# A macaron encoder block: another scheduling clock at a hand-over, five late tiles instead of four, the last norm's weights through another queue, and an uncut last piece

## The chip, the cores and the metric

The kernel runs on one core of a Trainium2 chip. The metric is the device time of one execution in microseconds (us), lower is better. The engines are TensorE (PE, matmuls; PEld is its weight load), VectorE (DVE), ScalarE (ACT), GpSimd (POOL) and SyncE (SP, which here only issues DMAs). Each runs its instructions in the order of its queue and waits there by semaphores.

## The reference

One layer on 1024 tokens of width 1024, in float32: a gated feed-forward half step, a mixer of three branches (sparse attention, a state-space layer, attention into a memory) that are gated, summed and projected, a second gated half step, and a last norm.

```python
x = x + 0.5 * swiglu_ffn(rms_norm(x, ffn1_norm[l]), ffn1_w_in[l], ffn1_w_out[l])
h = rms_norm(x, mix_norm[l])
...
x = x + merged @ w_out[l]
x = x + 0.5 * swiglu_ffn(rms_norm(x, ffn2_norm[l]), ffn2_w_in[l], ffn2_w_out[l])
x = rms_norm(x, final_norm[l])
```

`swiglu_ffn` is `(silu(h @ gate) * (h @ up)) @ w_out`, with 2816 hidden channels.

## The kernel before

**Matmuls.** The activations lie with channels on partitions; `xa` holds x, 8 tiles of 128 channels by 1024 tokens, in two halves of 512 tokens. Each matmul operand is a float16 number and a float16 remainder, and a product is three matmuls (`matmul3`, line 930).

**Weights.** A weight block is loaded into one of two float32 buffers (`wf`) by SP's queue. ACT squares it (`junk`, whose row sums are `wss`), PE adds these across partitions (`ms<-wss,ones_b`), DVE makes a scale of it (`wsc`), ACT writes the scaled float16 copy and DVE the remainder (both `wh`). Only then is `wf` free for the next load but one. `WBlock.steps` (line 235) is this list; `Stream.prep` puts the steps between the matmuls, each where an order's clock says that its engine has time.

**The order's clock.** `Model` (line 70) adds up a cost for every instruction as it is written, by engine and size (`cost`, line 102), and keeps from it a time per engine and per piece of memory. `Sched` and `Stream.prep` decide by these times what is written next, so costs and due times here move instructions in each engine's order, while the chip then runs the order as it stands. `WBlock.LATE` is how many us after its squares a block's sum over partitions may come. Tiles named in `nc.free` are left out of the clock; `xa` is among them during the mixer.

**The hand-over.** The mixer's output stage (`out_stage`, line 1165, called at line 2368) has 16 units of 24 matmuls, one per tile d of 128 channels and half of the tokens; DVE adds x to each (`xa<-mm`), ACT squares it (`sq`). `tail_order(8, 4)` takes both halves of tiles 0 to 3, then half 0 of tiles 4 to 7, then their half 1, so that half 0 is complete four units before the end. The generator `norm_forms` (line 865) then makes that half's norm, in four pairs of `xa<-xa,gs,ao` on DVE, and the float16 forms `F` and `FB` on ACT, DVE and POOL. The second FFN's `ffn_strassen` (line 1012) begins with six heads, three blocks of weights by two halves, of 96 matmuls of 256 columns each. Beside the heads, norm_forms makes sums of quarters of x (`xa<-xa`) and their forms. After them, 19 blocks go through a Strassen product; the sums of their weights (`wsum`) are POOL's. `ffn_strassen` sets the clock for this body behind the head loop:

```python
rows.apart, self.stream.BACKLOG = True, 2.0
nc.ACC, WBlock.LATE = {"scalar": 0.25, "vector": 0.08}, 1.0
```

**The end.** The last output stage (`out_stage` at line 2538) multiplies the FFN's hidden tiles (`H`, and the last ones in `xa`) with `w_out`. `final` (line 2372) turns each result back to tokens by rows (transposes into `lg`), multiplies it with the norm's weights (`F<-lg,xa`; the weights lie in a piece of `xa`, loaded by ACT's queue at line 2535), and after the last tile makes the root and scales the rows, which SP's queue stores 128 at a time. The last unit is cut in two pieces of 256 tokens (`cut=(0, HT // 2, HT)`); its 33 products are made twice with 256 columns, and root, scaling and stores follow each piece for two groups of 128 rows.

Of the kernel before, what the change touches and what calls it, by code (L numbers as in the profile page):

```python
# [17 lines left out]
P = 128  # L18
S = 1024
D = 1024  # L20
ND = D // P
HT = 512
# [29 lines left out]
class Engine:  # L52


    def __init__(self, model, name, engine):
        self.model, self.name, self.engine = model, name, engine
# [13 lines left out]
class Model:  # L70
# [6 lines left out]
    def __init__(self, nc):  # L77
        self.nc = nc
        self.t = {n: 0.0 for n in self.ENGINES}
        self.dma, self.end = 0.0, 0.0  # L80
        self.wrote, self.used, self.last, self.slots, self.ring, self.free = {}, {}, {}, {}, {}, set()
        for n in self.ENGINES:
            setattr(self, n, Engine(self, n, getattr(nc, n)))
# [18 lines left out]
    def cost(self, e, op, out, ins, acc):  # L102
        size = lambda a: a.free_size()
        n = max([size(out)] + [size(a) for a in ins]) if e != "tensor" else size(out)
        ptrs = sum(1 for a in ins[1:] if size(a) == 1 and n > 1)
        if e == "tensor":
            c = (n / 2400 + 0.0025) * (1 if ins[0].dtype != F32 else 4)
            return max(0.026, c * (0.6 if out.shape[0] <= 64 else 1.0))
        if e == "scalar":
            return 0.07 + n * 0.833e-3 + 0.093 * ptrs  # L110
        if op == "reciprocal":
            return 0.07 + 6.3e-3 * n
        sbuf = all(a.space == bass.MemoryType.SB for a in [out] + ins)
        fast = 0.52e-3 if op in ("tensor_scalar", "tensor_copy", "memset") and sbuf and not acc else 1.042e-3
        if e == "gpsimd":
            return 0.13 + n * (3.64e-3 if op == "tensor_scalar" else 2.0e-3)
        return 0.065 + n * fast + 0.061 * ptrs
# [269 lines left out]
class SBlock(WBlock):  # L387
# [40 lines left out]
    def sum(self):  # L428
        kb, nc, i = self.kb, self.kb.nc, self.summed
        H = self.HALF  # L430
        end, nc.end = nc.end, 0.0
        self.s[i] = kb.sums.tile([P, 2 * H], F32, name="wsum", tag=f"wsum{i}")
        x, y = self.s[i][:, 0:H], self.s[i][:, H:2 * H]
        sub = lambda o, a, b: nc.gpsimd.tensor_tensor(o, a, b, op=OP.subtract)
        if i == 0:
            nc.gpsimd.tensor_tensor(x, self.a(2), self.a(3), op=OP.add)
            sub(y, x, self.a(0))
        else:
            sub(x, self.a(0), self.a(2))
            sub(y, self.a(1), self.s[0][:, H:2 * H])  # L440
        self.summed += 1
        self.sums_at[i], nc.end = nc.end, end
# [162 lines left out]
class Builder:  # L605
# [406 lines left out]
    def ffn_strassen(self, name, rows, a, b, F, ring, early, chunks, xd):  # L1012
# [4 lines left out]
        nc = self.nc  # L1017
# [10 lines left out]
        def begin(f, c, tiles, gt):  # L1028
            w = a[f]
            yield from self.stream.begin(w, "head")  # L1030
            v = lambda g, j: g.rearrange("p (h a t) -> p a h t", h=2, a=2)[:, j, c.start // C:c.stop // C]
            return dict(w=w, c=c, gt=[v(gt, j) for j in range(2)], **dict(zip(("a", "u2", "u3", "si"), tiles)))
# [8 lines left out]
        def m1(s):  # L1041
            s["b1"] = self.mm()
            product(s, "b1", "A11", "B11", False)
            nc.scalar.activation(s["a"], s["b1"][:, s["c"]], AF.Copy)
# [69 lines left out]
        for i, (f, half) in enumerate(self.head_order(PLAIN)):  # L1114
            if i in (0, 2):
                yield f"h{name}.{half}"
            w = a[f]
# [16 lines left out]
                rows.put(f, gts[f])  # L1134
                rows.flush()
        rows.apart, self.stream.BACKLOG = True, 2.0
        nc.ACC, WBlock.LATE = {"scalar": 0.25, "vector": 0.08}, 1.0
        ends = [r1 for _, r1 in chunks[:-1]]

        def first(f):  # L1140
            if f == PLAIN:
                for half in range(2):
                    yield f"f{name}.{half}"
            gt = ring("gt")
            s = yield from begin(f, whole, [ring("post") for _ in range(4)], gt)
            m1(s)
            s["row"] = f, gt
            yield None
            return s
# [1061 lines left out]
    def mixer(self, w, xa, ss, xd_in, xd_out, after):  # L2211


        nc, tc, sched = self.nc, self.tc, self.sched
# [97 lines left out]
        for n in range(2 * ND):  # L2312
# [5 lines left out]
            gb, ga = self.bank("lg"), self.mm()  # L2318
# [43 lines left out]
        xo, F = after()  # L2362
        pool = m3.enter_context(tc.tile_pool(name="xo4", bufs=1, side="right"))
        xo = xo + [pool.tile([P, HT], F32, name="xo4", tag=f"xo4{i}") for i in range(3)]
        xo = iter([xo[i % len(xo)] for i in range(2 * ND)])
        for h in range(2):
            sched.add(self.norm_forms(xa, h, lambda h=h: self.row_sums(ss[h]), 2, "3", F), 0)
        yield from self.out_stage(w["out"], w["m"], lambda: next(xo), xd_in, 2, 4, self.keep_x("3", xa, ss, xd_out), 4)
        m3.close()

    def final(self, xt, ss, gb, out):
# [48 lines left out]
def tile_hybrid_block(ctx, tc, x, mem, ffn1_norm, ffn1_w_in, ffn1_w_out, mix_norm, w_in, a_q_gain, a_k_gain, rel_bias,  # L2420
# [4 lines left out]
    kb = Builder(ctx, tc)  # L2425
    nc, const, sched, stream = kb.nc, kb.const, kb.sched, kb.stream
    ctx.enter_context(kb.psum("ps", 2, 3, 2, 1))
    xa = const.tile([P, ND, 2, 2, HT // 2], F32, name="xa")
    nc.free.add(xa.tensor.name)
    ss = [const.tile([P, HT], F32, name=f"ss{h}") for h in range(2)]  # L2430
    xd = [kb.dram.tile([ND, 2, P, HT], F32, name=f"xd{i}") for i in range(3)]
# [7 lines left out]
    g1, g2 = Rows(kb, NF, "G"), Rows(kb, NF, "H")  # L2439
    a1, b1 = kb.ffn_blocks(ffn1_w_in[0], ffn1_w_out[0], 0, g1)  # L2440
    a2, b2, order2 = kb.sblocks(ffn2_w_in[0], ffn2_w_out[0], 2, g2, chunks)
# [45 lines left out]
    def main():  # L2487
        yield from kb.ffn_in("1", pa, a1, g1, xa, before)
        for h in range(2):
            sched.add(kb.norm_split(xa, h, lambda h=h: kb.row_sums(ss[h]), 1, "2"), 0)  # L2490
        xo = lambda: pa.tile([P, 2, HT], F32, name="xo", tag="gt", bufs=2)[:, 0]
        yield from kb.out_stage(b1, g1, xo, xd[0], 1, 2, kb.keep_x("2", xa, ss, xd[1]))
        st.close()
        with ExitStack() as en:
            F = {}

            def after():
                pool = en.enter_context(tc.tile_pool(name="g3", bufs=1, reuse_waits="tile"))
                F["pool"], F["B12", 0] = pool, pool.tile([P, ND // 2, 2, HT // 2], F16, name="FB12", tag="wsum1")
                names = ("B11", "B21", "B22", "T1", "T2", "T3", "T4")  # L2500
                F["all"] = pool.tile([P, len(names), ND // 2, 2, HT], F16, name="F")
                for i, n in enumerate(names):
                    F[n] = F["all"][:, i]
                F["xo"] = [pool.tile([P, HT], F32, name="xo3", tag=f"xo3{i}") for i in range(4)]
                return F["xo"], F

            yield from kb.mixer(mw, xa, ss, xd[1], xd[2], after)
            nc.free.discard(xa.tensor.name)
            pool = en.enter_context(tc.tile_pool(name="g4", bufs=1, reuse_waits="tile"))
            F["B12", 1] = pool.tile([P, ND // 2, 2, HT // 2], F16, name="FB12", tag="H7")  # L2510
            tiles = xa.rearrange("p k a h t -> p (k a h t)").rearrange("p (i t) -> p i t", t=HT)
            n = {"post": 0, "gt": 0, "xo": 0}

            def ring(kind):
                n[kind] += 1
                i = n[kind] - 1
                if kind == "xo":
                    return F["xo"][i % 4]
                if kind == "gt":
                    i = 8 + 2 * (i % 2)  # L2520
                    return tiles[:, i:i + 2].rearrange("p i t -> p (i t)")
                return tiles[:, i % 8]

            def room(k):
                k %= chunks[0][1]
                if k > 8:
                    i = 12 + 2 * (k - 9)
                    return tiles[:, i:i + 2].rearrange("p i t -> p (i t)").bitcast(F16).rearrange("p (j t) -> p j t", j=2)
                return pool.tile([P, 2, S], F16, name="H", tag=f"H{k}")

            g2.room = room
            early = lambda f: pool.tile([P, 2 * HT], F32, name="early", tag=f"H{4 + f}")
            yield from kb.ffn_strassen("3", g2, a2, b2, F, ring, early, chunks, xd[2])
            gb = tiles[:, 8:10].rearrange("p i t -> p (i t)")
            nc.scalar.dma_start(gb, final_norm.to_broadcast([P, D]))
            xt = F["all"].rearrange("p n k j t -> p (n k j t)").bitcast(F32)[:, 0:S * D // P].rearrange("p (i n) -> p i n", n=D)
            done, between = kb.final(xt, ss, gb, out[0])
            yield from kb.out_stage(b2[-1], g2, lambda: ring("xo"), xd[2], 2, 2, done, 3, cut=(0, HT // 2, HT), between=between)
            between()

    sched.add(setup(), 1)
    sched.add(main(), 3)
    sched.run()

# [29 lines left out]
```

## Time and profile before

| | |
|---|---|
| median of 3 runs | 2273.84 us (2272.67 to 2274.34) |
| the profiled execution | 2275.79 us, of which its span is 2273.9 |
| mean granted clock of PE | 0.980 |
| busy share of the span | PE 95%, DVE 60%, ACT 52%, POOL 18% |
| second output stage of the mixer and heads | about 1480 to 1659 us |
| Strassen body | 1659 to 1820 and 1937 to 2123 us, between them the first half of the second output product |
| last output stage and norm | 2123 to 2273.9 us |

Times in the rows are us from the start of the span. A row of a timeline has start, duration, engine, the line that emitted it (all go through a helper at line 62), operation, output tile<-inputs and shapes; in brackets the engine's idle time before it and what ended that. Buffer numbers are left out of names there. A row "x12" groups 12 like instructions, its duration is from the first's start to the last's end.

### The profile page before, as it was taken

The page shows a single profiled execution, that of the slowest core. Times are in us where ns is not written, and L with a number is a line of the kernel's source. Part 1 is how long each engine was busy: PE and PEld are TensorE (multiplying, and loading weights), DVE is VectorE, ACT ScalarE, POOL GpSimd, SP SyncE. Part 2 cuts the span into 40 slices and gives each one's busy share as a digit, 9 for nine tenths or more (in the row PEclk, how much of TensorE's full clock was granted, in tenths as well). Part 3 has the DMA queues.
Part 4 walks back from the last instruction along what each step waited for, and adds up shares of the span by engine and source line. Part 5 has one row for each costly group of instructions (what it writes and reads, how often), then busy time and mean ns, then how long its engine had stood idle before and what let it go on. Part 6 is the DMA issues. An engine that isn't in the chain of part 4 may idle for free. (4 is left out here: it accounts for less than half of the span.)

```text
span 2273.9 us, 33537 instructions
## 1 busy us (share of the span) xinstructions
PE 2155.2 (95%) x12618; PEld 1154.3 (51%) x12622; DVE 1353.6 (60%) x3682; ACT 1187.5 (52%) x2368; POOL 399.1 (18%) x581
## 2 busy tenths in 40 slices
PE   7999999999999889979999999898999999999897
PEld 4555444444444556666566674344844444444344
DVE  6446853345555476768669876775746643566553
ACT  6543433344444488778877675544445432455421
POOL 1200130000000014302200005400434301344000
PEclk9999999999999999989999999998999999999998
DMA  6422231202222112123322123244011233112212
GB/s 222 121 86 79 58 102 56 63 26 84 88 88 84 47 32 68 45 64 121 124 68 76 48 69 129 101 146 133 2 55 56 70 125 121 47 56 63 88 54 93
DMA packets 204067, 185.20 MB, mean 81 GB/s; under 512 B 7376, under 2 KB 176528, under 8 KB 203264
## 3 DMA queue, kind: packets, MB, share of 16 engines
q1 hardware_dynamic: 185904, 135.84, 18.9%
q0 software_dynamic: 8272, 28.84, 3.9%
q10 hardware_dynamic: 9728, 18.38, 2.6%
q8 instruction: 99, 1.62, 0.3%
q14 instruction: 64, 0.52, 0.1%
HBM read 143.57 MB, written 40.50 MB: 81 GB/s over the span
## 5 line engine op out<-in xcount | busy, mean ns | idle before, releaser
L62 PEld LDWEIGHTS <-wh 128*128 128x128 f16 x8445 | 824.8, 99 | 954.9 <-issue 41.1
L62 PE MATMUL mm<-xa,wh 128*128 128x512 f16 x2382 | 541.1, 380 | 6.5 <-ACT xa L62 4.9
L62 PE MATMUL lg<-xa,wh 128*128 128x512 f16 x1080 | 244.2, 381 | 0.4 <-DVE xn L62 0.4
L62 ACT ACTIVATE junk<-wf 128x1024 f16<-128x1024 f32 (+3 forms) x292 | 193.9, 664 | 39.3 <-DMA wf<-in_ffn_w_in_dram 22.3
L62 PE MATMUL mm<-G,wh 128*128 128x512 f16 x960 | 210.5, 379 | 0.0
L62 DVE SCALAR_TENSOR_TENSOR wh<-wf,wsc,wh 128x1024 f16<-128x1024 f32 (+1 forms) x132 | 178.4, 1355 | 53.0 <-ACT wh L62 52.9
L62 PE MATMUL mm<-H,wh 128*128 128x512 f16 (+1 forms) x891 | 199.9, 381 | 8.1 <-ACT wh L62 7.8
L62 PE MATMUL lg<-F,wh 128*128 128x512 f16 (+1 forms) x900 | 180.7, 355 | 0.0
L62 ACT ACTIVATE wh<-wf,wrs 128x128 f16<-128x128 f32 (+2 forms) x304 | 112.9, 438 | 99.8 <-DVE wrs L62 92.8
L62 ACT ACTIVATE wh<-wf,wsc 128x1024 f16<-128x1024 f32 (+1 forms) x132 | 139.1, 1059 | 39.5 <-DVE wsc L62 26.0
L62 PE MATMUL mm<-wh,xa 128*128 128x256 f16 (+2 forms) x1152 | 129.5, 272 | 12.8 <-ACT us L62 6.7
L62 PE MATMUL mm<-F,wh 128*128 128x512 f16 (+1 forms) x672 | 130.9, 351 | 5.7 <-DVE xa L62 4.0
L62 PEld LDWEIGHTS <-xa 128*128 128x128 f16 x1152 | 108.2, 106 | 30.9 <-issue 14.3
L62 DVE SCALAR_TENSOR_TENSOR wh<-wf,wrs,wh 128x128 f16<-128x128 f32 (+2 forms) x304 | 111.8, 419 | 14.8 <-ACT wh L62 13.6
L62 DVE SCALAR_TENSOR_TENSOR gt<-lg,wsc,si 128x512 f32<-128x512 f32 x44 | 33.0, 750 | 130.1 <-PE lg L62 111.0
L62 PE MATMUL ao<-F,wh 128*128 128x512 f16 x456 | 104.6, 379 | 0.0
L62 ACT ACTIVATE junk<-wk,kathr 128x1024 f16<-128x1024 f32 (+2 forms) x96 | 99.5, 1036 | 8.7 <-POOL kathr L62 6.8
L62 POOL TENSOR_TENSOR xa<-hs,xa 128x512 f16<-128x512 f32 x16 | 19.9, 1249 | 478.0 <-ACT xa L62 478.0
L62 DVE SCALAR_TENSOR_TENSOR xo<-mm,wsc,xo 128x512 f32<-128x512 f32 x44 | 33.0, 750 | 112.0 <-PE mm L62 112.0
L62 POOL TENSOR_TENSOR xa<-xa 128x512 f32<-128x512 f32 (+1 forms) x40 | 58.0, 1452 | 173.9 <-ACT xa L62 168.1
L62 ACT ACTIVATE junk<-gt 128x1024 f16<-128x1024 f32 x22 | 23.2, 1056 | 116.5 <-DVE gt L62 116.5
L62 ACT ACTIVATE si<-mm,wsc 128x512 f32<-128x512 f32 x50 | 33.9, 677 | 92.7 <-PE mm L62 80.9
(510 smaller groups left out, 2993.4 us busy)
## 6 DMA issues: line engine op xcount, KB each, us to landing
wf<-in_ffn_w_in_dram SPq DMA_DIRECT2D x88, 512.0 KB, 4.8
xo<-xd ACTq DMA_DIRECT2D x64, 256.0 KB, 2.7
gd<-gt SPq DMA_DIRECT2D x48, 256.0 KB, 2.0
xa<-gd POOLq DMA_DIRECT2D x16, 768.0 KB, 5.1
wf<-in_ffn_w_out_dram SPq DMA_DIRECT2D x8, 1280.0 KB, 5.8
wf<-in_ffn_w_out_dram SPq DMA_DIRECT2D x7, 1408.0 KB, 6.1
wf<-in_w_in_dram SPq DMA_DIRECT2D x17, 512.0 KB, 4.8
xd<-xa SPq DMA_DIRECT2D x32, 256.0 KB, 2.4
```

What stands on the lines that cost most here:

```text
L62: r = f(*a, **k)
```

## The change

Five edits. The clock gets a factor `shared` for sums of two operands in SBUF on DVE and POOL; it is set to 1.6 behind the head loop of the second FFN and back to 1.0 when both halves' forms are there. `LATE` for the body goes from 1.0 to 2.5. The mixer's output stage takes both halves of tiles 0 to 2 only, then half 0 of tiles 3 to 7, then half 1 of these (five late tiles). The last norm's weights are loaded by GpSimd's queue. The last unit is not cut.

```diff
--- before.py
+++ after.py
@@ -77,7 +77,7 @@
     def __init__(self, nc):
         self.nc = nc
         self.t = {n: 0.0 for n in self.ENGINES}
-        self.dma, self.end = 0.0, 0.0
+        self.dma, self.end, self.shared = 0.0, 0.0, 1.0
         self.wrote, self.used, self.last, self.slots, self.ring, self.free = {}, {}, {}, {}, {}, set()
@@ -112,6 +112,8 @@
             return 0.07 + 6.3e-3 * n
         sbuf = all(a.space == bass.MemoryType.SB for a in [out] + ins)
         fast = 0.52e-3 if op in ("tensor_scalar", "tensor_copy", "memset") and sbuf and not acc else 1.042e-3
+        if op == "tensor_tensor" and sbuf and e != "scalar":
+            n *= self.shared
         if e == "gpsimd":
             return 0.13 + n * (3.64e-3 if op == "tensor_scalar" else 2.0e-3)
         return 0.065 + n * fast + 0.061 * ptrs
@@ -1134,13 +1136,15 @@
                 rows.put(f, gts[f])
                 rows.flush()
         rows.apart, self.stream.BACKLOG = True, 2.0
-        nc.ACC, WBlock.LATE = {"scalar": 0.25, "vector": 0.08}, 1.0
+        nc.ACC, WBlock.LATE = {"scalar": 0.25, "vector": 0.08}, 2.5
+        nc.shared = 1.6
         ends = [r1 for _, r1 in chunks[:-1]]
 
         def first(f):
             if f == PLAIN:
                 for half in range(2):
                     yield f"f{name}.{half}"
+                nc.shared = 1.0
@@ -2365,7 +2369,7 @@
-        yield from self.out_stage(w["out"], w["m"], lambda: next(xo), xd_in, 2, 4, self.keep_x("3", xa, ss, xd_out), 4)
+        yield from self.out_stage(w["out"], w["m"], lambda: next(xo), xd_in, 2, 5, self.keep_x("3", xa, ss, xd_out), 4)
         m3.close()
@@ -2532,10 +2536,10 @@
             gb = tiles[:, 8:10].rearrange("p i t -> p (i t)")
-            nc.scalar.dma_start(gb, final_norm.to_broadcast([P, D]))
+            nc.gpsimd.dma_start(gb, final_norm.to_broadcast([P, D]))
             xt = F["all"].rearrange("p n k j t -> p (n k j t)").bitcast(F32)[:, 0:S * D // P].rearrange("p (i n) -> p i n", n=D)
             done, between = kb.final(xt, ss, gb, out[0])
-            yield from kb.out_stage(b2[-1], g2, lambda: ring("xo"), xd[2], 2, 2, done, 3, cut=(0, HT // 2, HT), between=between)
+            yield from kb.out_stage(b2[-1], g2, lambda: ring("xo"), xd[2], 2, 2, done, 3, between=between)
```

The places where engines' orders change and on which the prediction speaks:

**ACT, at the mixer's last units.** `sq` squares a finished unit, `junk` a weight block, `F` and `FB` are half 0's forms; blocks are numbered by buffer. Before, with block 2 of `w_in` in `wf_15948`:

```order
L62 DMA xo4_15400<-xd1_95 128x512
L62 ACTIVATE sq_16009<-xa_91 128x512
L62 ACTIVATE junk_16026,wss_16025<-wf_15948 128x1024
L62 ACTIVATE junk_16034,wss_16025<-wf_15948 128x1024
L62 DMA xo3_15391<-xd1_95 128x512
L62 ACTIVATE sq_16072<-xa_91 128x512
L62 ACTIVATE wh_16075<-wf_15896,wsc_15987 128x1024 x2
L62 ACTIVATE F_15390<-xa_91 128x2x256
L62 ACTIVATE FB12_15389<-xa_91 128x2x256
L62 ACTIVATE F_15390<-xa_91 128x2x256
L62 ACTIVATE FB12_15389<-xa_91 128x2x256
L62 ACTIVATE F_15390<-xa_91 128x2x256 x2
```

Now, with block 2 in `wf_16011`:

```order
L62 ACTIVATE sq_16034<-xa_91 128x512
L62 ACTIVATE F_15390<-xa_91 128x2x256
L62 ACTIVATE FB12_15389<-xa_91 128x2x256
L62 ACTIVATE F_15390<-xa_91 128x2x256
L62 ACTIVATE FB12_15389<-xa_91 128x2x256
L62 ACTIVATE F_15390<-xa_91 128x2x256 x4
L62 DMA xo3_15391<-xd1_95 128x512
L62 ACTIVATE sq_16089<-xa_91 128x512
L62 ACTIVATE wh_16105<-wf_15863,wsc_15946 128x1024
L62 ACTIVATE junk_16115,wss_16114<-wf_16011 128x1024
L62 ACTIVATE junk_16117,wss_16114<-wf_16011 128x1024
L62 DMA xo3_15392<-xd1_95 128x512
```

Block 2's two square sums stood ahead of half 0's forms; now they stand behind all of them, behind the square of unit 13 (`sq_16089`) and a weight copy of block 1.

**PE, the sum of these squares over partitions.** Before, in unit 13 (`mm_16012`, the fourteenth being the next), after 18 of its 24 matmuls, with half 0's norm sums behind it:

```order
L62 MATMUL mm_16012<-m_15139,wh_15698 128x512
L62 LDWEIGHTS ones_b_76
L62 MATMUL ms_16037<-wss_16025,ones_b_76 128x1
L62 MATMUL ms_16043<-ones_74,ss0_92 128x1 x4
L62 LDWEIGHTS wh_15698
L62 MATMUL mm_16012<-m_15256,wh_15698 128x512
```

Now, in unit 14 (`mm_16092`, the last but one) after 18 of its 24:

```order
L62 LDWEIGHTS wh_15822
L62 MATMUL mm_16092<-m_15139,wh_15822 128x512
L62 LDWEIGHTS ones_b_76
L62 MATMUL ms_16120<-wss_16114,ones_b_76 128x1
L62 LDWEIGHTS wh_15822
L62 MATMUL mm_16092<-m_15256,wh_15822 128x512
```

The sum moved from unit 13 to unit 14; the units are counted from 0 to 15. Half 0's norm sums (`ss0`) went one unit forward.

**DVE, at the end of the hand-over.** `H` is the exit of a head, `wh<-wsum` and `wh<-wf` are remainders of block 3, whose buffer `wf_16208` the load of block 5 takes next. Before:

```order
L62 SCALAR_TENSOR_TENSOR H_16709<-early_16177,rsc_16708,H_16709 128x1024
L62 SCALAR_TENSOR_TENSOR wh_16650<-wsum_16497,wsc_16242,wh_16650 128x1024
L62 TENSOR_TENSOR F_15390<-xa_91,F_15390 128x4x256
L62 SCALAR_TENSOR_TENSOR wh_16823<-wf_16208,wsc_16242,wh_16823 128x512
L62 SCALAR_TENSOR_TENSOR early_16178<-lg_16719,wsc_16036,si_16827 128x512
L62 SCALAR_TENSOR_TENSOR wh_16823<-wsum_16526,wsc_16242,wh_16823 128x1024
```

Now:

```order
L62 SCALAR_TENSOR_TENSOR H_16712<-early_16180,rsc_16711,H_16712 128x1024
L62 SCALAR_TENSOR_TENSOR wh_16590<-wsum_16499,wsc_16291,wh_16590 128x1024
L62 SCALAR_TENSOR_TENSOR wh_16799<-wf_16208,wsc_16291,wh_16799 128x512
L62 SCALAR_TENSOR_TENSOR wh_16799<-wsum_16502,wsc_16291,wh_16799 128x1024
L62 SCALAR_TENSOR_TENSOR early_16181<-lg_16722,wsc_16119,si_16834 128x512
```

The remainder that reads `wf_16208` followed a form `F`; now it follows the remainder of the sums directly.

**ACT, at the start of the last output stage.** One piece of the difference:

```order
 L62 ACTIVATE junk,rsc<-xa 128x1024
 L62 ACTIVATE xa<-xa,rsc 128x1024
-L62 DMA xa<-in_final_norm_dram 128x1024
 L62 DMA xo_15391<-xd_96 128x512
 L62 DMA xo_15392<-xd_96 128x512
-L62 ACTIVATE wh<-wf,wrs 128x256 x5
-L62 ACTIVATE junk,wrq<-wf 128x256 x3
-L62 ACTIVATE wh<-wf,wrs 128x256 x2
-L62 ACTIVATE junk,wrq<-wf 128x256
+L62 ACTIVATE wh<-wf,wrs 128x256 x7
+L62 ACTIVATE junk,wrq<-wf 128x256 x4
```

The load of the norm's weights is gone from ACT's queue (it is the last DMA in POOL's), and two weight copies that came ahead of this piece are in it now.

## Rows read from the trace of the kernel before

**Rows 1.** Waits of PE, 1560 to 1660 us: engine, line, releaser: us, times, longest
```profile
PE ms L62 <- ACT junk L62: 13.0, 4, 6.4
```

**Rows 2.** Timeline of PE, 1540 to 1585 us: start, us, instruction [idle before <-releaser]
```profile
1558.92 0.60 PE L62 MATMUL ao<-ident,ny 128*128 128x128 f32 x4
...
1571.28 3.66 PE L62 MATMUL mm<-F,wh 128*128 128x256 f16 x19 [3.99 <-DVE xa L62]
...
1582.84 0.16 PE L62 MATMUL ms<-wss,ones_b 128*128 128x1 bf16 x1 [4.15 <-ACT junk L62]
```

**Rows 3.** Chain of waits, 1555 to 1662 us: start, us, what
```profile
1647.41 4.97 DMA wf<-in_ffn_w_in_dram
1652.46 1.16 ACT junk L62 x2
1653.82 5.14 PE lg L62 x24
```

**Rows 4.** Table by stretches: us, busy time of each engine, PEclk, DMA share, GB/s
```profile
1446.00:1478.00 32.00, 26.30 (x119) 11.29 (x118) 21.92 (x42) 18.78 (x36) 14.69 (x11) 1.00 0.32 108
1660.00:1820.00 160.00, 160.00 (x753) 72.72 (x752) 97.81 (x153) 81.44 (x124) 63.90 (x44) 1.00 0.19 58
```

**Rows 5.** Timeline of DVE, 1555 to 1662 us
```profile
1562.36 1.40 DVE L62 SCALAR_TENSOR_TENSOR xa<-xa,gs,ao 128x512 f32<-128x512 f32 x2
...
1565.07 1.40 DVE L62 SCALAR_TENSOR_TENSOR xa<-xa,gs,ao 128x512 f32<-128x512 f32 x2
...
1597.47 1.39 DVE L62 SCALAR_TENSOR_TENSOR xa<-xa,gs,ao 128x512 f32<-128x512 f32 x2
...
1622.70 1.21 DVE L62 TENSOR_TENSOR xa<-xa 128x1024 f32<-128x1024 f32 x1
...
1641.24 3.14 DVE L62 TENSOR_TENSOR F<-xa,F 128x1024 f16<-128x1024 f32 x1
1644.30 2.61 DVE L62 SCALAR_TENSOR_TENSOR wh<-wf,wsc,wh 128x512 f16<-128x512 f32 x1
```

**Rows 6.** Timeline of POOL, 1600 to 1650 us
```profile
1640.18 6.19 POOL L62 TENSOR_TENSOR F<-xa,F 128x1024 f16<-128x1024 f32 x2
```

**Rows 7.** Timelines of ACT and then of PE, 2114 to 2141 us
```profile
2127.93 1.15 ACT L62 ACTIVATE xa<-xa,rsc 128x1024 f16<-128x1024 f32 x1 [0.41 <-DVE rsc L62]
2130.49 0.34 ACTq L62 DMA_DIRECT2D xa<-in_final_norm_dram  x1
...
2131.85 2.10 ACT L62 ACTIVATE wh<-wf,wrs 128x256 f16<-128x256 f32 x5 [2.77 <-issue]
...
2132.41 2.74 PE L62 MATMUL mm<-H,wh 128*128 128x512 f16 x6 [6.52 <-ACT wh L62]
...
2135.02 5.21 PE L62 MATMUL mm<-H,wh 128*128 128x512 f16 x18
```

**Rows 8.** Timelines of PE and then of ACT, 1995 to 2020 us
```profile
2008.90 0.19 PE L62 MATMUL ms<-wss,ones_b 128*128 128x1 bf16 x2
...
2018.28 1.13 ACT L62 ACTIVATE wh<-wf,wsc 128x1024 f16<-128x1024 f32 x1
```

**Rows 9.** The page's DMA issues, and the timeline of DVE, 2150 to 2158 us
```profile
xa<-gd POOLq DMA_DIRECT2D x16, 768.0 KB, 5.1
...
2153.26 0.68 DVE L62 TENSOR_TENSOR F<-lg,xa 128x512 f32<-128x512 f32 x1
```

**Rows 10.** Timelines of PE, DVE and SP's queue, 2240 to 2274 us
```profile
2243.02 0.60 PE L62 MATMUL lg<-ident,xn 128*128 128x128 f32 x4
...
2253.33 4.77 PE L62 MATMUL mm<-H,wh 128*128 128x256 f16 x27
...
2248.23 2.08 DVE L62 TENSOR_SCALAR F<-F,ny 128x1024 f32<-128x1024 f32 x3
...
2268.05 0.75 DVE L62 TENSOR_SCALAR F<-F,ny 128x1024 f32<-128x1024 f32 x1
...
2249.01 20.63 SPq L62 DMA_DIRECT2D out_dram<-F  x8
```

## Prediction

> **What bounds the kernel now.** I read the page first: TensorE (PE) is busy 95% of the span and granted full clock almost everywhere, so only places where PE stops, or runs slowly after a stop, can give time back. The waits of PE by window show where: between 1560 and 1660 us, where the mixer hands over to the second FFN, it waits 13.0 us in four stops for square sums of weights (`ms` behind ACT's `junk`) [rows 1], and 4.0 us at the first head for a PSUM bank that VectorE (DVE) still reads; the timeline shows the bank at 1571.28 and the first square sum, 4.15 us, at 1582.84 [rows 2]. The last and longest stop, 6.4 us [rows 1], ends the hand-over. The chain of waits tells why: the load of block 5 (the sixth block of `w_in`) leaves only at 1647.0, takes 4.97, its second square ends at 1653.6, and the 24 short matmuls after it, of 256 columns, take 5.14 us [rows 3]. That is 0.214 each, what one of 512 columns takes at a granted 1.00 [rows 4]: the stop has cost half the clock, and at full clock they take 2.57. What holds the load is DVE: its queue must make the last low part that reads block 3's buffer, 2.61 us at 1644.30, behind an `F` sum of 3.14 us at 1641.24; that shape takes 1.21 when alone [rows 5]. GpSimd (POOL) runs two sums at the same time [rows 6].
>
> Elsewhere PE has nothing to give: between 1660 and 1820 it is busy 160.00 of 160.00 us, 753 matmuls of 512 columns but for the few small ones, 0.2125 us each [rows 4]. At the start of the final output stage it waits 6.52 us for ACT [rows 7].
>
> **The change part by part.**
>
> *The 1.6.* Both halves of every sum are counted longer only after the head loop is written. The orders with and without this line have the same rows on every engine, so it is 0: no row moves.
>
> *Later square sums in 16 body units.* `ms` moves 12 matmuls back, 12 × 0.2125 = 2.6 us. In the unit at 2008.90 the scale that comes of it is first used by ACT at 2018.28 [rows 8]; DVE makes it within 2 us of `ms`, so some 7 us are left, and 2.6 fit. Cost 0. If the cover were gone, each unit would pay what is over; nothing in the rows says so.
>
> *Five late tiles: the hand-over.* Half 0 now closes one unit earlier. Transposes stood at 1558.92 [rows 2]; one unit of 24 is 5.1, so about 1553.8, and 0.4 of short waits make 1554.2. The first norm pair followed 3.44 later, pairs step by 2.71 [rows 5], so the four pairs last from 1557.6 to 1568.4. Behind them DVE has the exit of unit 13 and ACT its square (some 0.7 each, half of a pair's 1.40 [rows 5]), one weight copy (1.13 [rows 8]) and then block 2's two squares (1.16 each [rows 3]): 4.8 in sum, 1573.2. In the new order `ms` for these squares stands in PE's unit 14 after 18 of 24 matmuls. The old unit 14 began two units before 1567.3 (the start at 1571.28 less its wait of 3.99 [rows 2]), at 1557.1; 18 matmuls make 1560.9. Following ACT's regrouped copies through units 7 to 12 gives five more stops of 0.2 to 1.0, 2.6 together; they could be none. So PE stands still from 1563.5 to 1573.2: **a new wait of 9.7 us**. After the 6.5 us stop at 2132, 24 matmuls took 7.8 (to 2140.2) where 5.1 is normal [rows 4, 7], so 2.7 more for the clock. The head starts at 1573.2 + 30 × 0.2125 + 2.7 = 1582.3, 11.0 later than now.
>
> Against this, what follows no longer stops. Half 1's pairs stand on DVE behind a block's scale: now that of block 4, at 1597.47 [rows 5]; in the new order that of block 3, which PE reaches 72 short matmuls (7.7) and two small groups (2.0) after the head's start, about 1592.3: **5.2 us earlier**, though PE began 11.0 later. Another product's exit between the pairs and a stop of some 2 us at block 4's sum eat 2.7, so the low parts begin 2.5 earlier. At the end the `F` sum (3.14) is no longer between DVE's last steps; it is paid earlier at about the same price, and the low part may go from 2.61 to half of that, since POOL is by then done. So the load leaves 2.5 to 5.0 us earlier; I take 4.2, nearest the case where 2.61 shrinks but not wholly. PE arrives at block 5's sum at 1646 to 1647.5 (552 short matmuls after 1582.3, with 4 us of small groups and the one stop), and the sum is there at 1649.5: a stop of about 2.5 in the place of 6.4. Between 1446 and 1478 PE stood 5.7 of 32 us in short stops at a granted 1.00 [rows 4], so I give back 1.8 of the 2.57 that the last head lost. Hand-over: −4.2 − 1.8 = **−6.0**. Bounds: PE not waiting for block 5 at all, 1647 + 2.6 against 1659.0 (1653.82 + 5.14): −9.3; the load as late as now: 0.
>
> Here a page bears on the price. DVE's `F` sum took 3.14 beside POOL's pair of 6.19, and 1.21 without [rows 5, 6]. The Trainium skill, "SBUF — State Buffer", section "Who interferes with whom", says that DVE and GpSimd share one port pair as an exclusive lock: the loser waits for a whole instruction; the rows agree in size (1.21 plus most of one of POOL's 3.1). By a strict lock the low part would stay long, the load would leave 3.1 earlier and the clock give 0.9, so −4.0 in the place of −6.0 and 2268.5 in all.
>
> *Weights by POOL's queue, first copies later.* ACT ends its scaled exit at 2129.1 and then spends until 2131.85 on three DMA issues, the first waiting for DVE to free the buffer; without that one it starts its copies near 2130.0, 1.8 earlier [rows 7]. But PE goes into the wait with 6 matmuls fewer done, 1.3: **−0.4** (bounds −1.8 and 0; no row of ACT's sets more). The issue now waits on POOL, where nothing is queued behind it. POOL's 768 KB issue takes 5.1, so the weights are there by 2136; DVE first reads them at 2153.26 [rows 9]. 17 us of cover: 0.
>
> *Last piece uncut.* 66 matmuls of 256 columns become 33 of 512: the same time. Sums stand after 18 of them, as now, until 2253.33; the 15 others, at half clock first, end near 2258.4. Then one chain over four rows: exit, transposes, four squares, root, scaling. Half 0's took 7.3 from transposes (2243.02) to the last scaling (2248.23 + 2.08), so 2266.8 where the second piece's last scaling ends at 2268.05 + 0.75 [rows 10]. But all four rows' stores, 2 MB at the some 420 GB/s that stores reach, 5.0 us, now start together, near 2266.3, and end at 2271.3; now two rows go ahead, SP's last issue ends at 2269.6 [rows 10], and the span 4.3 later. With the same 1.7 after the last byte: 2273.0 against 2273.9, **−0.9**. Bounds: −2.7 if stores overlap the chain, +1 if the wider chain delays the first store by 2.
>
> Sum: 0 + 0 − 6.0 − 0.4 − 0.9 = −7.3. The profiled execution took 2275.79, so 2268.5; it stands 1.95 over the median of the runs, so **2266.5**. About 0.2% (4.5 us) is what a measurement here tells from no change.
>
> **The rivals.**
>
> *A: the new wait is carried on (slower).* A weight buffer is freed only when its copies are made, so a late block 2 delays the loads of blocks 3, 4 and 5. Block 3's load leaves behind a copy that now follows unit 14's exit. If the ring of two buffers hands this on, block 5's load leaves as late as PE is, not when DVE is done: the new 9.7 + 2.7 stand, and of today's stops only the bank's 4.0 and its clock (1.5), and one square stop (about 0.6), go: +6.3, less 1.3 for the end of the kernel, +5.0: 2278.8. It decides if the load leaves after 1652. For it: 9.7 is as long as two loads. Against: half 1's pairs, which hold the load now, come earlier.
>
> *B: no gain at the hand-over (same).* The `F` sums taken out of DVE's last steps push others in front of the low part, and the load leaves at 1647.0 as now. Then only −1.3 is left: 2272.5. It decides at a load after 1646. For it: DVE's work between 1597 and 1647 is the same in sum. Against: 5.2 us of earlier start, and the two engines' stretched instructions.
>
> *C: the tail loses.* Stores that ran ahead under the second piece's chain are bunched; +1 with the rest as forecast: 2268.4, still faster.
>
> *D: the short stops in units 7 to 12 don't come,* and PE need not wait for block 5: 2262 to 2263.
>
> **How the numbers follow.** The forecast with C and D 0.62, its own range 2261.5 to 2269.5; B 0.22; A 0.16. The range takes in the lowest bound (−9.3, −0.4, −2.7: 2261.4) and all of B (2272.5, with +1 and the tail at no gain 2275); of A it leaves out most. Faster 0.62, same 0.22, slower 0.16.
>
> **What would show it.** In the changed profile: one PE wait of 8 to 11 us at `ms` in the last but one unit of the mixer's output stage, near 1563; no wait for a bank at the first head; half 1's first pair on DVE at 1591 to 1594; block 5's load issued at 1642 to 1644, and a stop under 3 us behind it; PE without waits in the body; ACT's copies resuming near 2130 less the shift; one chain after the last matmul and the last store issued within 3 us of the first of its group. I am wrong if the load of block 5 leaves at 1646 or later, or if unit 14's wait is over 13.

## The result and the profile after

The changed kernel takes 2260.48 us (median of 4 runs, 2257.12 to 2262.78), the kernel before 2274.09 beside it (4 runs, 2272.67 to 2274.9). The ratio is 0.994, interval 0.9922 to 0.9957: 13.6 us faster, where 7.3 were forecast, and 0.5 us under the low end of the range, 2261. The direction and the place were right, the size was not.

The profiled execution took 2257.12 us, 3.4 under its median, so its trace is compared by stages and not by its end. The page's first lines, the same as stood for the kernel before with a span of 2273.9:

```profile
span 2255.0 us, 33448 instructions
...
PE 2140.5 (95%) x12585; PEld 1141.1 (51%) x12589; DVE 1347.8 (60%) x3669; ACT 1186.8 (53%) x2367; POOL 396.2 (18%) x582
```

| stage (marks on PE) | before | after | forecast |
|---|---|---|---|
| start to the mixer's output stage (first `lg<-m` of 18) | 1497.38 | 1492.44 | no change |
| from there to the first Strassen matmul | 161.38 | 152.65: **−8.7** | −6.0 |
| Strassen body and first output half, to the first `mm<-H` of the last stage | 464.38 | 463.84: −0.5 | 0 |
| last stage, to its first `lg<-xa` | 26.66 | 24.58: **−2.1** | −0.4 |
| from there to the last norm sums | 102.61 | 102.61 | 0 |
| last norm sums to the end of the span | 21.49 | 18.88: **−2.6** | −0.9 |

The first row, 4.9 us in a part that has the same instructions in the same order, is the spread of single executions, not the change: between 900 and 1200 us the granted clock was 0.97 before and 0.99 after. The other five rows sum to −14.0, near the 13.6 of the medians.

**The hand-over.** Waits of PE from 1540 to 1660, as [rows 1] for before (engine, line, releaser: us, times, longest):

```profile
PE ms L62 <- ACT junk L62: 10.9, 5, 7.7
```

One line of waits before a matmul is left, and no wait for a bank. Timeline of PE, answering [rows 2] (start, us, instruction [idle before <-releaser]):

```profile
1565.73 0.16 PE L62 MATMUL ms<-wss,ones_b 128*128 128x1 bf16 x1 [7.75 <-ACT junk L62]
1566.91 0.16 PE L62 MATMUL ms<-wss,ones_b 128*128 128x1 bf16 x1 [1.02 <-ACT junk L62]
1566.94 9.49 PE L62 MATMUL mm<-m,wh 128*128 128x512 f16 x30
1576.27 2.78 PE L62 MATMUL mm<-F,wh 128*128 128x256 f16 x24
...
1642.45 0.16 PE L62 MATMUL ms<-wss,ones_b 128*128 128x1 bf16 x1 [0.19 <-ACT junk L62]
1642.47 1.47 PE L62 MATMUL lg<-FB,wh 128*128 128x256 f16 x12
```

The new stop in unit 14 is there: 7.75 + 1.02, 8.8 us where 9.7 were forecast, and the 30 matmuls behind it take 9.49 where 30 like them take 6.63 at full clock (at 1547.58 in the trace before). With the 4.9 us of the first row added, the first head starts at 1581.2 (forecast 1582.3). But block 5's stop is 0.19 us, not 2.5, and the 24 short matmuls behind it run at full speed, 1.47 for each 12. The chain of waits, answering [rows 3], says why:

```profile
1634.59 1.28 POOL wsum L62
1635.88 0.37 SPq L62
1636.30 4.86 DMA wf<-in_ffn_w_in_dram
...
1642.61 2.64 PE lg L62 x24
```

The load leaves at 1635.9, which is 1640.8 on the scale of before: 6.2 us earlier, where I had 4.2 and a bound of 5.0. In this trace it is released by POOL's weight sum and no longer by DVE. DVE and POOL, answering [rows 5, 6]:

```profile
1586.32 1.40 DVE L62 SCALAR_TENSOR_TENSOR xa<-xa,gs,ao 128x512 f32<-128x512 f32 x2
...
1624.58 2.35 DVE L62 TENSOR_TENSOR F<-xa,F 128x1024 f16<-128x1024 f32 x2
...
1630.36 1.28 DVE L62 SCALAR_TENSOR_TENSOR H<-early,rsc,H 128x1024 f16<-128x1024 f32 x1 [0.96 <-ACT H L62]
1631.57 1.28 DVE L62 SCALAR_TENSOR_TENSOR wh<-wsum,wsc,wh 128x1024 f16<-128x1024 f32 x1
1632.76 0.74 DVE L62 SCALAR_TENSOR_TENSOR wh<-wf,wsc,wh 128x512 f16<-128x512 f32 x1
```

```profile
1609.84 2.14 POOL L62 TENSOR_TENSOR wsum<-wsum,wf 128x512 f32<-128x512 f32 x1
1633.17 1.46 POOL L62 TENSOR_TENSOR wsum<-wf 128x512 f32<-128x512 f32 x1 [21.19 <-PE lg L62]
1634.59 1.27 POOL L62 TENSOR_TENSOR wsum<-wf,wsum 128x512 f32<-128x512 f32 x1
1635.81 5.20 POOL L62 TENSOR_TENSOR F<-xa,F 128x1024 f16<-128x1024 f32 x2
```

Half 1's first pair stands at 1586.32, 1591.3 on the scale of before, 6.2 earlier (forecast 5.2). The last two `F` sums cost 1.2 each at 1624.58, where POOL does nothing (from 1612.0 to 1633.2); before, the last one cost 3.14 beside POOL's sums. The exit `H` ahead of the two remainders stands at 1630.36, which is 2.5 earlier than before, and behind it the remainders take 1.28 and 0.74 where before they took 2.30 and 2.61. So DVE is done with block 3's buffer at 1633.5, 8.5 earlier on the scale of before; then POOL's weight sum holds it 2.4 us more. That sum reads the same buffer and starts at 1633.17; the profile names `lg` matmuls of PE as what released it.

Granted clock of PE (us, busy times, PEclk, DMA share, GB/s): low behind unit 14's stop, full at the end of the hand-over. In the first Strassen part PE has no wait, as before [rows 4]; in the whole body its waits are 2.5 us in sum in both traces.

```profile
1566.00:1577.00 11.00, 10.09 (x38) 4.32 (x38) 3.69 (x7) 2.53 (x4) 0.00 (x0) 0.69 0.15 48
1640.00:1646.00 6.00, 5.81 (x52) 4.76 (x51) 1.07 (x4) 3.35 (x6) 5.92 (x5) 1.00 0.13 39
```

**The last output stage**, answering [rows 7, 9], PE, then ACT, POOL's issue and the first use of the weights on DVE:

```profile
2110.28 1.04 PE L62 MATMUL mm<-H,wh 128*128 128x512 f16 x4 [0.75 <-DVE wh L62]
2115.18 0.79 PE L62 MATMUL mm<-H,wh 128*128 128x512 f16 x2 [3.87 <-ACT wh L62]
2116.57 4.75 PE L62 MATMUL mm<-H,wh 128*128 128x512 f16 x16 [0.60 <-DVE wh L62]
```

```profile
2113.58 1.15 ACT L62 ACTIVATE xa<-xa,rsc 128x1024 f16<-128x1024 f32 x1 [0.41 <-DVE rsc L62]
2114.63 2.89 ACT L62 ACTIVATE wh<-wf,wrs 128x256 f16<-128x256 f32 x7
...
2116.42 0.61 POOL L62 DMA_DIRECT2D xa<-in_final_norm_dram  x1 [4.44 <-DVE xa L62]
...
2136.97 0.68 DVE L62 TENSOR_TENSOR F<-lg,xa 128x512 f32<-128x512 f32 x1
```

PE's stops sum to 5.2 (before 6.52), and 18 matmuls take 5.5 us behind them. ACT's two issues no longer wait, and its copies start right behind its exit. The weights are issued 20.6 us ahead of their first use.

**The end**, answering [rows 10], PE:

```profile
2236.12 1.05 PE L62 MATMUL ms<-ones,ss 128*128 128x1 f32 x8 [0.73 <-DVE ss L62]
2237.03 2.10 PE L62 MATMUL mm<-H,wh 128*128 128x512 f16 x9
```

Nine matmuls of 512 columns take 2.10 behind the norm sums: here PE stays at full clock. Before, 27 short ones took 4.77 at this place, and 27 took 3.11 at 2246.69, at full clock.

### The profile page after: what moved, and what is told of

The parts are those of the page before. It is cut to its first block, busy times and chain, and to the rows that moved or that the text cites. A ratio compares the mean times of both kernels' runs of the same rounds, so it can differ in the third digit from the quotient of the medians.

```text
span 2255.0 us, 33448 instructions
## 1 busy us (share of the span) xinstructions
PE 2140.5 (95%) x12585; PEld 1141.1 (51%) x12589; DVE 1347.8 (60%) x3669; ACT 1186.8 (53%) x2367; POOL 396.2 (18%) x582
## 5 line engine op out<-in xcount | busy, mean ns | idle before, releaser
L62 PE MATMUL mm<-H,wh 128*128 128x512 f16 x864 | 197.3, 383 | 6.8 <-ACT wh L62 5.2
L62 PE MATMUL mm<-m,wh 128*128 128x512 f16 x336 | 79.9, 395 | 5.1 <-DVE wh L62 3.2
```

The source lines that it names most:

```text
L62: r = f(*a, **k)
```

## The experiments

All stages below are from one trace each, in the order of the table above: hand-over, body, last stage, end. Ratios are against runs of the kernel before beside each run; the first row has its median beside the changed kernel, beside the other runs it was 2272.9 to 2273.2.

| run | median us | ratio to before (interval) | hand-over | body | last stage | end |
|---|---|---|---|---|---|---|
| before | 2274.09 | | 161.4 | 464.4 | 26.7 | 21.5 |
| changed | 2260.48 | 0.994 (0.9922 to 0.9957) | 152.7 | 463.8 | 24.6 | 18.9 |
| only_five | 2261.79 | 0.9951 (0.9938 to 0.9965) | 150.8 | 462.3 | 26.3 | 21.5 |
| only_late | 2272.46 | 0.9997 (0.9989 to 1.0006) | 161.3 | 464.3 | 27.9 | 19.6 |
| only_gb | 2269.72 | 0.9984 (0.9975 to 0.9992) | 160.1 | 463.6 | 23.4 | 19.7 |
| only_uncut | 2273.62 | 0.9999 (0.9991 to 1.0008) | 161.0 | 464.2 | 26.6 | 20.6 |
| factor_off | 2260.15 | 0.9944 (0.9933 to 0.9956) | 152.1 | 463.6 | 24.4 | 19.0 |
| no_late | 2262.76 | 0.9954 (0.994 to 0.9967) | 152.5 | 463.9 | 25.2 | 20.6 |
| t4_on_pool | 2270.31 | 0.9995 (0.9985 to 1.0004) | 158.1 | 464.4 | 26.6 | 21.5 |
| sums2_later6 | 2259.23 | 0.9944 (0.9929 to 0.9958) | 151.3 | 464.0 | 26.4 | 19.0 |
| sums2_later8 | 2255.06 | 0.9925 (0.9912 to 0.9937) | 145.4 | 464.0 | 26.4 | 18.9 |
| sums2_later8_late1 | 2256.51 | 0.9923 (0.9911 to 0.9935) | 146.5 | 462.3 | 23.4 | 19.0 |
| later8_late1_pace1 | 2256.07 | 0.9933 (0.9921 to 0.9944) | 148.6 | 463.6 | 23.4 | 18.9 |
| six_tiles | 2268.49 | 0.9979 (0.997 to 0.9987) | 158.1 | 464.0 | 25.2 | 20.6 |

### One edit at a time

**Five late tiles alone.**

```diff
-        yield from self.out_stage(w["out"], w["m"], lambda: next(xo), xd_in, 2, 4, self.keep_x("3", xa, ss, xd_out), 4)
+        yield from self.out_stage(w["out"], w["m"], lambda: next(xo), xd_in, 2, 5, self.keep_x("3", xa, ss, xd_out), 4)
```

> The kernel before with five late tiles alone; LATE, the weights' queue, the cut and the factor stay as before. Theory: the hand-over's gain is this edit's alone. The order of all engines between the mixer's output stage and the first Strassen unit is that of the changed kernel, so the 8.7 us that its trace shows there (Strassen starts 13.7 earlier, of which 4.9 were there before the stage began) and the 0.4 of clock behind it come whole: ratio 0.996, -8 to -10 us; one PE stop of 8 to 9 us at the square sum of block 2 and next to none at block 5. Rival: the later LATE or the factor is part of it, and this run gives under 5 us.

It gives 0.9951, 11 us: the hand-over's gain is this edit's alone. Its trace shows 10.5 in the hand-over and not 8.7, most of the difference because the clock came back sooner behind the same stops: the 30 matmuls that took 9.49 above take 7.97 here.

```profile
1570.75 0.16 PE L62 MATMUL ms<-wss,ones_b 128*128 128x1 bf16 x1 [7.75 <-ACT junk L62]
...
1571.96 7.97 PE L62 MATMUL mm<-m,wh 128*128 128x512 f16 x30
```

**LATE 2.5 alone.**

```diff
-        nc.ACC, WBlock.LATE = {"scalar": 0.25, "vector": 0.08}, 1.0
+        nc.ACC, WBlock.LATE = {"scalar": 0.25, "vector": 0.08}, 2.5
```

> The kernel before with LATE 2.5 in place of 1.0 alone. Theory: nothing in the 16 body units; at the start of the last output stage ACT makes seven weight copies in one row behind its DMA issues, PE has 6 matmuls fewer done when it stops: between -0.5 and +1.5 us. Rival: this edit is what gave 2.1 us there, and the run shows -2 by itself.

No difference that can be measured; in the trace the last stage is 1.2 longer (27.86 against 26.66), as the theory has it, and the body as long as before.

**The weights by GpSimd's queue alone.**

```diff
-            nc.scalar.dma_start(gb, final_norm.to_broadcast([P, D]))
+            nc.gpsimd.dma_start(gb, final_norm.to_broadcast([P, D]))
```

> The kernel before with the last norm's weights by GpSimd's queue alone. Theory: ACT no longer waits for DVE ahead of its weight copies; PE's stop of 6.5 us at the start of the last output stage becomes 3.5 to 5, and less of the clock is lost: -2 to -4 us. Rival: the issue was hidden and the time stays within 1 us.

0.9984, 3.6 us, as expected, and 3.3 in the last stage of the trace: PE's stop of 6.52 becomes 3.64 + 0.35.

```profile
2128.36 1.03 PE L62 MATMUL mm<-H,wh 128*128 128x512 f16 x2 [3.64 <-ACT wh L62]
2129.75 1.89 PE L62 MATMUL mm<-H,wh 128*128 128x512 f16 x4 [0.35 <-DVE wh L62]
```

**The last unit uncut alone.**

```diff
-            yield from kb.out_stage(b2[-1], g2, lambda: ring("xo"), xd[2], 2, 2, done, 3, cut=(0, HT // 2, HT), between=between)
+            yield from kb.out_stage(b2[-1], g2, lambda: ring("xo"), xd[2], 2, 2, done, 3, between=between)
```

> The kernel before with the last unit uncut alone. Theory: 2.6 us, as in the changed kernel's trace: 1.7 because PE stays at full clock behind the stop at the norm's sums, 0.9 as forecast. Rival: the clock falls there in this kernel too, and it is 0.9 or less.

The theory of 2.6 falls. The runs show no difference, and the trace shows the rival: here PE is slow behind the same norm sums, and the end takes 20.6.

```profile
2248.80 3.78 PE L62 MATMUL mm<-H,wh 128*128 128x512 f16 x9
```

With the last piece cut, only_gb kept the clock at this place and its end took 19.7:

```profile
2248.92 3.11 PE L62 MATMUL mm<-H,wh 128*128 128x256 f16 x27
```

So the clock falls in some executions of either kernel. With the clock down the end takes 21.5 cut (before, only_five, t4_on_pool) and 20.6 uncut (only_uncut, no_late, six_tiles); with the clock up 19.6 and 19.7 cut, 18.9 to 19.0 uncut. The edit is worth 0.6 to 0.9 in the traces, near the forecast; the other 1.7 of the changed kernel's trace came with the clock. By their ratios the four edits alone add up to −15.7 us, and the changed kernel gained 13.6; with intervals of 2 to 3 us to either side of each the runs cannot tell these apart.

**Without the factor 1.6.**

```diff
-        if op == "tensor_tensor" and sbuf and e != "scalar":
-            n *= self.shared
...
-        nc.shared = 1.6
...
-                nc.shared = 1.0
```

> The changed kernel without the factor 1.6: the same instructions in the same order on every engine. Theory: the same time as the changed kernel, and its spread shows how much runs of one order differ: median within 2 us of 2260.5, ratio to the kernel before 0.994 within 0.0015. Rival: the line matters in a way that the order doesn't show, and it is 3 us or more away.

2260.15 against 2260.48, ratio 0.9944 against 0.994: the factor does nothing, as the order said.

**All but LATE.** The changed kernel with 1.0 in the line of LATE.

> The changed kernel with LATE back at 1.0. Theory: the later square sums cost 1.2 us at the start of the last output stage (PE has 6 matmuls fewer done when it stops for ACT; with LATE alone the stage from its first matmul to its first product of xa took 27.9 us, before 26.7) and nothing elsewhere: 1 to 2 us faster than the changed kernel, that stage about 23.4 us. Rival: the parts overlap, and it is the same or slower.

2262.76, within its spread of the changed kernel, so the 1 to 2 us expected are not seen. The last stage took 25.2 and not 23.4: the stops are those of only_gb, but the clock fell. In the traces with LATE 1.0 it took 23.4 or 25.2, with 2.5 it took 24.4 to 24.6 or 26.35, so LATE costs 1.15 there either way, and whether the clock falls decides 1.8. The medians don't show 1.15.

### Why block 5's load left earlier

**One form's low part on POOL, in the kernel before.**

```diff
         lo = parts("T4", X(1, 0))
         yield pace(0.5)
-        lo(nc.vector)
+        lo(nc.gpsimd)
```

> The kernel before, with the low part of one form (T4) made by GpSimd and not by VectorE; nothing else is changed, half 1's pairs start as before. It takes the sum of 3.14 us out of DVE's queue ahead of the low part that holds block 5's load. Theory: that sum is about half of the 6.2 us by which block 5's load left earlier in the changed kernel: the load leaves 2 to 4 us earlier, PE's last stop goes from 6.4 to 3 to 4, and the kernel is 2 to 4 us faster than before. Rival: the earlier start of half 1's pairs is all of it, or POOL's longer queue takes it back: within 1 us of before.

DVE, POOL:

```profile
1639.99 2.28 DVE L62 SCALAR_TENSOR_TENSOR wh<-wsum,wsc,wh 128x1024 f16<-128x1024 f32 x1
1642.19 2.61 DVE L62 SCALAR_TENSOR_TENSOR wh<-wf,wsc,wh 128x512 f16<-128x512 f32 x1
```

```profile
1641.15 8.71 POOL L62 TENSOR_TENSOR F<-xa,F 128x1024 f16<-128x1024 f32 x3
```

The load leaves at 1644.9, 3.0 earlier on the scale of before (this trace reaches the output stage 0.9 later), PE's first stop of the two goes from 6.35 to 3.02, and the hand-over is 3.3 shorter. So taking the `F` sum out of DVE's way is worth about half of the 6.2, as the theory has it, in the trace; the 2 to 4 us that were expected of the whole kernel are not shown, since the ratio is 0.9995 with an interval that holds 1. DVE's remainders stay long, 2.28 and 2.61, beside POOL's three sums.

That these remainders became short is not the other half. In only_five the engines have the changed kernel's order here, but PE is 1.5 us earlier, so that POOL's weight sum starts beside the remainders and not behind them. DVE, POOL:

```profile
1635.08 2.29 DVE L62 SCALAR_TENSOR_TENSOR wh<-wsum,wsc,wh 128x1024 f16<-128x1024 f32 x1
1637.29 1.75 DVE L62 SCALAR_TENSOR_TENSOR wh<-wf,wsc,wh 128x512 f16<-128x512 f32 x1
```

```profile
1635.01 1.28 POOL L62 TENSOR_TENSOR wsum<-wf 128x512 f32<-128x512 f32 x1 [19.52 <-PE lg L62]
```

The remainders are long, DVE releases the load again, and it leaves at 1639.1, 8.0 earlier than before (this trace reaches the output stage 0.1 later). What the traces with the new order share is that the `F` sum no longer stands between DVE's last steps and that the exit `H` ahead of these stands earlier, by 2.5 to 4.0 us.

### What the new stop costs

**Block 2's sum later.** One line behind the making of the blocks; in the first run 6.0, in the second 8.0:

```diff
+    a2[2].LATE = 8.0
```

> The changed kernel, but block 2 alone has its square sum due 6 us after its squares, which puts it behind the last matmul of unit 15. Theory: the stop of 8.8 us in unit 14 and the 1.5 to 3 us of half clock behind it are a true cost: PE then waits some 3.6 for the bank of unit 13 and 1 for the sum, the first head starts 5 to 8 us earlier, and the kernel is 3 to 6 us faster than the changed one. Rival: what follows is bound by DVE's pairs and the loads, the stop was idle time that comes back later (at half 1's pairs or at block 5), and the time stays within 1.5 us.

> As the run with 6 us, but due 8 us after the squares, which puts block 2's sum behind the first 24 matmuls of the first head; block 2's copies, and with them the load of block 4, come 2 to 3 us later. Theory of a true stop: 3 to 6 us faster than the changed kernel, within 2 of the run with 6 us. Rival, loads bind: slower than the run with 6 us by the delay of its loads, 2 to 4 us.

With 6 the first head starts 5.4 us earlier but the hand-over ends only 1.3 earlier, and the time is the changed kernel's: its rival has the time right. With 8 the hand-over is 7.3 shorter and the kernel 0.9925, which is 3.4 us under the changed one by the ratios and 5.4 by the medians; each of its runs (2250.8 to 2256.3) is under each run of the changed kernel and of factor_off, which has the same order (2257.1 to 2262.8). PE, first with 6, then with 8:

```profile
1566.98 7.96 PE L62 MATMUL mm<-m,wh 128*128 128x512 f16 x24 [3.71 <-DVE xa L62]
...
1639.63 0.16 PE L62 MATMUL ms<-wss,ones_b 128*128 128x1 bf16 x1 [2.84 <-ACT junk L62]
1641.11 0.16 PE L62 MATMUL ms<-wss,ones_b 128*128 128x1 bf16 x1 [1.31 <-ACT junk L62]
1641.13 2.72 PE L62 MATMUL mm<-FB,wh 128*128 128x256 f16 x12
```

```profile
1567.67 6.73 PE L62 MATMUL mm<-m,wh 128*128 128x512 f16 x24 [3.71 <-DVE xa L62]
...
1639.88 0.16 PE L62 MATMUL ms<-wss,ones_b 128*128 128x1 bf16 x1 [1.33 <-ACT junk L62]
1639.91 1.47 PE L62 MATMUL lg<-FB,wh 128*128 128x256 f16 x12
```

In both the stop in unit 14 is gone and unit 15 waits 3.71 for its bank. The load of block 5 is late in neither: counted from the start of the output stage it leaves 5.5 us earlier than in the changed kernel with 6, and 7.2 earlier with 8. The difference lies in PE's order at the end. With 6, block 5's sum stands 24 short matmuls further ahead: 48 of them follow it and not 24, which is 2.6 us at full clock. PE comes to it sooner, stops 2.84 + 1.31, and behind that the clock falls, 1.4 us more. With 8 the sum has its old place, the stop is 1.33 and the clock holds. So the stop in unit 14 was a true cost, and with 6 most of it comes back because the one due time moved another block's sum as well. The rival by which later copies of block 2 delay the loads fell. Why block 5's load leaves 1.8 sooner with 8 than with 6 is not shown.

**8 us and LATE 1.0.** The line above in the kernel no_late.

> The changed kernel with block 2's square sum due 8 us late and LATE back at 1.0. Theory: LATE costs 1.15 us at the start of the last output stage, whether the clock falls there or not (24.6 against 23.4 and 26.35 against 25.2 in the traces so far): 1.1 us faster than with 8 us and LATE 2.5, so 2253 to 2255. Rival: within the spread of the runs it is not seen, or the body needs the later sums and it is slower.

Ratio 0.9923 against 0.9925: the same within the spread, as its rival has it. The last stage is 23.4, with the clock up.

**The pairs paced closely as well.**

```diff
-            yield pace() if half else pace(4.0)
+            yield pace() if half else pace(1.0)
```

> As the kernel with 8 us and LATE 1.0, and half 0's pairs follow the clock of the order closely (1.0 for 4.0 us), which puts the exit of unit 13 ahead of the fourth pair on DVE. Theory: PE's wait of 3.71 us for unit 13's bank shrinks by a pair, 2.7, to about 1, and less of the clock is lost: 2 to 4 us faster than without. Rival: the fourth pair is needed by the first head or half 1's chain is bound by loads, and it stays within 1 us.

```profile
1563.79 5.34 PE L62 MATMUL mm<-m,wh 128*128 128x512 f16 x24 [1.01 <-DVE xa L62]
1570.27 2.78 PE L62 MATMUL mm<-F,wh 128*128 128x256 f16 x24 [1.14 <-DVE xa L62]
1576.45 1.86 PE L62 MATMUL ms<-ones,ss 128*128 128x1 f32 x8 [3.38 <-DVE ss L62]
```

The bank wait shrinks by 2.7 as expected, and a wait of 3.38 for half 1's norm sums and one of 1.14 take its place: 0.9933, no gain. The rival's time came, by a wait that neither theory named: DVE's sums of squares (`ss`) are later.

**Six late tiles** (and LATE 1.0).

```diff
-        yield from self.out_stage(w["out"], w["m"], lambda: next(xo), xd_in, 2, 5, self.keep_x("3", xa, ss, xd_out), 4)
+        yield from self.out_stage(w["out"], w["m"], lambda: next(xo), xd_in, 2, 6, self.keep_x("3", xa, ss, xd_out), 4)
```

> The changed kernel with LATE 1.0 and six late tiles in place of five. Half 0 closes one more unit early, and the clock puts block 2's square sum behind the first 24 matmuls of the first head by itself. Theory: the gain of five tiles is half 1's earlier pairs and comes whether or not there is a stop in unit 14; without that stop it is 3 to 7 us faster than the changed kernel, as with 8 us. Rival: half 1, now six units in a row, closes no earlier and ACT's copies of the output weights come too late for the units before, so it is slower than the changed kernel.

0.9979: 8 us slower than the changed kernel by the medians and 5.7 slower than no_late, from which it differs by the sixth tile alone. Block 2's sum stops PE no more, but PE waits 4.98 for a bank ahead of unit 14. Half 1's first pair is early; its second stands behind block 4's scale, which PE makes only after a stop of 3.48 (PE, then DVE).

```profile
1562.08 12.63 PE L62 MATMUL mm<-m,wh 128*128 128x512 f16 x48 [4.98 <-DVE xa L62]
...
1592.64 0.16 PE L62 MATMUL ms<-wss,ones_b 128*128 128x1 bf16 x1 [3.48 <-ACT junk L62]
```

```profile
1586.98 1.40 DVE L62 SCALAR_TENSOR_TENSOR xa<-xa,gs,ao 128x512 f32<-128x512 f32 x2
...
1594.41 1.40 DVE L62 SCALAR_TENSOR_TENSOR xa<-xa,gs,ao 128x512 f32<-128x512 f32 x2
```

This fits a gain of five tiles that comes from half 1's pairs standing behind the scale of block 3, with nothing of block 4 between them. It does not show it alone, since the bank wait came in too and the two remainders ahead of block 5's load are long again, 2.29 and 2.62.

## Why the prediction was too small

- **The stop in unit 14**, 9.7 + 2.7: right, 8.8 and 1.3 to 2.9 over the runs. The five short stops in units 7 to 12, put at 2.6, were two of 0.61.
- **Half 1's pairs 5.2 earlier:** right, 6.2.
- **The load of block 5, −4.2: here the prediction failed.** The step was that the `F` sum "is paid earlier at about the same price". It cost 1.2 and not 3.14, since the new order sets it where POOL is idle. With that and the shorter remainders DVE was done with the buffer 8.5 earlier; POOL's weight sum, which the prediction did not price, held it for 2.4 of these, and the load left 6.2 earlier, beyond the bound of 5.0. The lock of the Trainium skill, "SBUF — State Buffer", section "Who interferes with whom", would have told this, had I asked which POOL instructions stand beside DVE's at the new place. I used it only to price the overlap, not to see it end. The traces agree with it: the sums and remainders are long wherever POOL's sums stand beside them, as in t4_on_pool, and short where POOL is idle.
- **The clock behind block 5's stop, −1.8:** PE came to block 5's sum at 1647.0 on the scale of before, as forecast, but the sum was there 2 us sooner, and with a stop of 0.19 all of 2.57 came back. Hand-over −8.7 in the place of −6.0; a further 0.4 at the first Strassen matmuls counts in the body. Over the traces with this order the hand-over took 150.8 to 152.7, over those with the old one 160.1 to 161.4.
- **The last stage, −0.4:** the size is right where the clock falls (26.35 against 26.66), but in the changed kernel's trace it stayed up, another 1.8. The parts were opposed: LATE, put at 1.3, cost 1.15 in the traces; the queue, put at 1.8, gave 3.6 by the runs and 3.3 in the trace, where PE's stop shrank by 2.5 and the clock was back sooner. I gave no price to that clock and no chance to its staying up.
- **The end, −0.9:** right at like clock, 0.6 to 0.9. The 1.7 more in the changed kernel's trace is luck with the clock.
- **The 1.6 and the body:** 0, right.
- **The rivals.** A's time did not come: the load left at 1640.8, not after 1652. A part of its mechanism did: the load follows PE, since without unit 14's stop it leaves 5.5 and 7.2 us earlier than in the changed kernel (sums2_later6, sums2_later8) where the first head starts 5.4 and 6.7 earlier. B did not come, nor did C. D nearly did: two short stops in the place of five, and 0.19 of wait for block 5. The range's low end, 2261.4, summed the bounds of hand-over and end but left the last stage at −0.4; with its own bound of −1.8 it would have been 2260.0 (and the bound of −9.3 is 9.4 by its own terms).

What stays open is why the clock falls behind a stop in one execution and not in the next; no run here tells. The changed kernel's own trace has it up in the last stage and at the end, where other traces with the same edits have it down, so these two rows of its table, −2.1 and −2.6, are on the lucky side.

## What to carry to other kernels

When an order moves an instruction of two engines that stretch each other, price it at its new place by what the other engine does there, and price its old neighbours again as well. A due time that is moved for one block can move others: the same stop taken away gave 3 to 5 us when the last sum kept its place in PE's order, and nothing when it came 24 matmuls sooner, so read the whole new order before a run is taken as the price of one step. Where several edits meet one stop, run each alone: here a gain of 3.6 hid a cost of about 1.

## What the runs showed of the hardware that was not expected

Behind equal stops of PE the granted clock stays down for different times, or does not fall at all. After the same stops of 7.75 and 1.02 us, 30 matmuls that take 6.63 at full clock took 9.49, 9.52, 8.95 and 7.97 in four traces, with a mean granted clock of 0.69 in the first and 0.83 in the last; after the same 0.73 before the last norm sums, 27 short ones took 3.11 (only_late, only_gb; granted clock 1.00 in the second) or 4.57 to 4.77 (only_five, before; 0.62 in the second). That is 1.5 to 1.8 us at a place, and several places a run: executions of one order spread over 3 to 8 us, so one trace may not be compared with another by its end.
